# Modulation vectors of the attention stages moved from TensorE to VectorE, in one queue through ten stages, with half of one projection placed between two attention heads

## The chip, the cores and the metric

One core of a Trainium2 chip runs the whole program. The metric is device microseconds of one execution, the median of several runs. TensorE (PE in the profile; PEld is its weight load) does the matmuls, VectorE (DVE) and ScalarE (ACT) the elementwise work, and SyncE (SP) issues the loads from HBM. Each engine works its own instructions off in one fixed order.

## The reference, cut to what matters

Two networks run one after the other on x of 256 tokens by 1024 features, in ten stages. The first has two layers of feed-forward, attention, feed-forward; the second two layers of mixer, feed-forward. Every stage i has the same frame:

```
sh, sc, g = split(silu(c) @ w_mod + b_mod)           # vectors of 1024
h = rms_norm(x) * gain * (1 + sc) + sh
x = x + g * block(h)
```

So the program needs 30 vectors of 1024 numbers, sh, sc and g of ten stages, and each is a product of a vector of 1024 with a 1024x1024 matrix of 4 MB. They hang on c alone, not on x, and can be worked out at any time before their use. An attention block has six latent heads (queries and keys are expanded from a narrow latent), six local heads (a window of 128 with a bias table, two key heads) and four stick-breaking heads; their outputs are normed by branch and projected by w_out.

## The kernel before

**Weights.** Every projection streams its weight through `wblocks` (lines 177 to 207) in blocks of 128 partitions by 1024 numbers. Line 186 issues the load of a block into a `raw` buffer; there are six of these, and feed-forward stages from the second on have six more (`rawx`). ScalarE rounds the block to `whi` (line 197), VectorE takes the rest `wlo = raw - whi` (line 198), and TensorE multiplies with both halves: lines 218, 231 and 235 where the weight is stationary (24 matmuls of 256 columns a block), 262, 263 and 265 where the activation is (12 matmuls of up to 512 columns a block). A feed-forward stage has 66 such blocks, a mixer 64.

**Vectors.** The matrix of one vector comes as eight row blocks ("rows" from here on) of 128x1024, 512 KB each, through the same `raw` buffers (line 437). `queue_vec` (from line 429) has two ways to use a row. In mode "dve" VectorE does `acc = acc + cond[k] * row`, line 452 for the first row and 454 for the others, and after eight rows `vec_row` sums over partitions with four matmuls against ones (line 481). In mode "pe" TensorE does the whole sum: four matmuls of 32 output rows by 256 columns for each row (line 447), all into the one PSUM bank `gv`. The profile counts each of these fp32 matmuls as two instructions, so eight for a row. In both modes ScalarE copies the sum to `vrow` (line 488), two matmuls transpose it (line 496), and VectorE adds the bias (line 500): `finish_vec`. The set-up's two vectors use "pe", the two attention stages use "pe" as well, all others "dve".

**Pacing.** `stage` queues a stage's vectors, and `pace` is called after each weight block and takes as many rows as keep them evenly spread: from block 4 to block 53 of a feed-forward, to block 57 of a mixer. The stages use 24, 24, 32, 24, 16, 32, 24, 24, 24 and 0 rows, 224 in all. In attention the pacing is by hand: after each head's second half `advance` takes three rows (`f3`) or one (`f1`), and `q` in `PLAN` takes what is left.

**Attention** (from line 1223). Projections come first; the local heads' projection of 512 columns (`proj_n(win, (416, 928), op)`, four blocks) stands between `up_proj` and `mla_prep`, which norms, rotates and transposes the latent queries and keys. Then `PLAN` orders the heads: `m` a latent head and `s` a local one, `S` the local heads' preparation `swa_prep`, `B` a branch's norm and transposition, `a` and `b` parts of the w_out projection, `d` how many heads are kept open. Each head has a first half (scores, maximum, exponential) and a second half (transposes, weighted sum).

```
PLAN = "d2 f3 m0 m1 d3 S B2 s0 f1 s1 s5 m3 m2 s3 s4 s2 a6 m4 m5 w B1 a4 b6 q B0 b4"
```

The order in which each engine gets its instructions is made by a scheduler: an instruction that stands later in the program can be put ahead of one that waits, as far as its buffers allow.

Of the kernel before, what the change touches and what calls it, by code (L numbers as in the profile page):

```python
# [9 lines left out]
F32 = mybir.dt.float32  # L10
# [27 lines left out]
PFFN = 53  # L38
PATT = 18
PLAN = "d2 f3 m0 m1 d3 S B2 s0 f1 s1 s5 m3 m2 s3 s4 s2 a6 m4 m5 w B1 a4 b6 q B0 b4"  # L40
PRE = (0, 0, 0, 0)
DEPTH = 3
PMIX = 57
GAIN_EARLY = (3, 4, 6, 7, 8, 9)
# [4 lines left out]
SH_MODE = "pe"  # L49
# [8 lines left out]
AHEAD_MORE = 4  # L58
AHEAD_PE = 1
# [72 lines left out]
class Net:  # L132
    def __init__(self, ctx, tc, A, out, offs, dbg=None):
# [11 lines left out]
        self.more, self.nraw, self.finishing = None, 0, None  # L145

# [240 lines left out]
    def stage(self, nblk, vecs, mode="dve", quiet=0, flush=False, apart=True, ahead=AHEAD):  # L387

        self.drain()
        for v in vecs:  # L390
            self.queue_vec(mode, *v, apart=apart)
        if apart:
            self.finish_last()
        elif flush:
            self.loads.append(None)
            self.steps.append(self.finish_last)
        self.total, self.ahead = len(self.steps), ahead
        self.done, self.nload, self.nblk, self.iblk = 0, 0, max(1, nblk - quiet), -quiet
        if ahead > AHEAD:
            self.preload(ahead)  # L400
# [5 lines left out]
    def next_step(self):  # L406

        self.preload(self.done + 1 + self.ahead)
        self.steps.pop(0)()
        self.done += 1  # L410
# [7 lines left out]

    def pace(self):
        if self.manual:  # L420
            return
        if self.later and self.iblk >= T5_WAIT and self.iblk % T5_EVERY == 0:
            self.later.pop(0)()
        self.iblk += 1
        want = min(self.total, -(-self.iblk * self.total // self.nblk))
        while self.done < want:
            self.next_step()

    def queue_vec(self, mode, w, col0, cond, cols, kind, key, apart):
# [3 lines left out]
        def load(b):  # L433
            raw = self.raw()
            m = LD // D
            rv = raw.rearrange("p (k n) -> p k n", k=m)
            nc.sync.dma_start(rv, w[b * P : (b + m) * P, col0 : col0 + D].rearrange("(k p) n -> p k n", p=P))
            for k in range(m):
                st[b + k] = rv[:, k, :]

        def use(b):
            if b == 0:
                st["acc"] = self.t(self.vp, [P, D], F32, "acc", 2) if mode == "dve" else self.gv()
            acc, row, k = st["acc"], st.pop(b), b
            if mode == "pe":
                for g in range(4):
                    nc.tensor.matmul(  # L447
                        acc[32 * g : 32 * g + 32, 0:S], lhsT=self.cond[cond][1][:, k, :], rhs=row[:, g * S : (g + 1) * S],
                        start=k == 0, stop=k == 7,
                    )  # L450
            elif k == 0:
                nc.vector.tensor_scalar(out=acc, in0=row, scalar1=self.cond[cond][0][:, 0:1], scalar2=None, op0=ALU.mult)
            else:
                nc.vector.scalar_tensor_tensor(  # L454
                    out=acc, in0=row, scalar=self.cond[cond][0][:, k : k + 1], in1=acc, op0=ALU.mult, op1=ALU.add
                )
            if b == 7:
                st["row"] = self.vec_row(mode, acc)
                if not apart:
                    self.finishing = lambda bank: self.finish_vec(st["row"], cols, kind, key, bank)  # L460

        for b in range(8):
# [515 lines left out]
    def stage_vecs(self, i):  # L978
# [5 lines left out]
        if i in GAIN_EARLY:  # L984
            keys = keys[1:]
# [797 lines left out]
```

## Time and profile before

| | |
|---|---|
| median of 3 runs | 1904.32 us |
| runs | 1897.71 to 1905.79 us |
| profiled execution, its own time | 1893.67 us |
| its span, first to last instruction | 1891.9 us |
| PE busy | 97% of the span |
| DVE busy | 72% |
| ACT busy | 51% |
| attention stages, about | 245 to 375 us and 766 to 890 us |
| mixers, about | 1090 to 1308 us and 1492 to 1710 us |

The profile shows one execution. Busy shares are means over stages with different limits. A matmul's end is modelled, so the time that a run of matmuls takes of PE is read from start to start. PEclk is the clock that TensorE was granted, as a share of 2.4 GHz: 1.00 or 0.50.

### The profile page before, as it was taken

How to read it: one execution, taken by the hardware profiler on the slowest of the kernel's cores; microseconds unless marked ns; L12 is line 12 of the kernel's file. 1: busy time of each engine (PE TensorE's matmuls, PEld its weight loads, DVE VectorE, ACT ScalarE, POOL GpSimd, SP SyncE). 2: the span in 40 equal slices, each digit the busy share in tenths (PEclk: the TensorE clock that was granted, in tenths of full speed). 3: DMA queues.
4: the chain of work that ended last, by engine and by line, in shares of the span. 5: the costliest groups of instructions: out<-in, count | busy, mean ns of one | idle time of the engine just before them, and what ended most of it. 6: DMA issues, size and time to landing. Idle time of an engine off the chain costs nothing.

```text
span 1891.9 us, 37147 instructions
## 1 busy us (share of the span) xinstructions
PE 1839.9 (97%) x15125; PEld 1736.0 (92%) x15125; DVE 1371.3 (72%) x2171; ACT 960.2 (51%) x1527; POOL 0.2 (0%) x4
## 2 busy tenths in 40 slices
PE   7999999999999999999999999999999999999998
PEld 5899996899999999968999988999999888999998
DVE  4897576698669765768986696679865777577554
ACT  3444475554445444756544454546444545455443
POOL 0000000000000000000000000000000000000000
PEclk8999999999999999999999999999999999999999
DMA  9698545789857963458798477578984585775550
GB/s 319 195 331 288 187 141 191 267 279 378 283 178 274 319 230 118 135 190 296 249 340 269 157 250 235 195 233 281 337 267 147 189 295 178 248 252 186 195 191 23
DMA packets 229447, 440.72 MB, mean 233 GB/s; under 512 B 15590, under 2 KB 79708, under 8 KB 229276
## 3 DMA queue, kind: packets, MB, share of 16 engines
q1 hardware_dynamic: 227740, 436.96, 68.0%
q8 instruction: 118, 1.93, 0.4%
q10 hardware_dynamic: 1536, 1.39, 0.2%
q14 instruction: 53, 0.43, 0.1%
HBM read 436.06 MB, written 2.23 MB: 232 GB/s over the span
## 4 chain that ended last, share of the span: by engine, by line
PE 87%; DVE 6%; DMA 3%; ACT 2%; issue 1%; SPq 0%; DVEq 0%; ACTq 0%
PE mm L218 24%; PE mm L235 23%; PE mm L231 23%; DVE wlo L198 2%; PE mm L262 2%; PE mm L265 2%; PE mm L263 2%; PE gv L447 2%; PE sm L771 1%; ACT whi L197 1%; DMA raw<-in_w_ffn_gu_dram 1%; PE mm L771 1%; PE gv L481 1%; DMA rawx<-in_w_mod_dram 1%; DMA raw<-in_w_mod_dram 1%
## 5 line engine op out<-in xcount | busy, mean ns | idle before, releaser
L218 PE MATMUL mm<-oph,whi 128*128 128x256 f32 (+1 forms) x3072 | 786.3, 282 | 13.3 <-DVE dly L302 4.9
L231 PE MATMUL mm<-opl,whi 128*128 128x256 f32 (+1 forms) x3072 | 780.0, 280 | 0.1
L197 ACT ACTIVATE whi<-raw 128x1024 fp32r<-128x1024 f32 (+2 forms) x408 | 426.2, 1047 | 455.4 <-PE mm L231 352.1
L198 DVE TENSOR_TENSOR wlo<-raw,whi 128x1024 fp32r<-128x1024 f32 (+2 forms) x408 | 489.8, 1208 | 176.5 <-ACT whi L197 168.5
L218 PEld LDWEIGHTS mm<-oph,whi 128*128 128x128 f32 x3072 | 582.5, 190 | 30.1 <-issue 10.3
L231 PEld LDWEIGHTS mm<-opl,whi 128*128 128x128 f32 x3072 | 582.6, 190 | 2.2 <-issue 0.9
L235 PE MATMUL mm<-oph,wlo 128*128 128x256 f32 (+1 forms) x3072 | 574.8, 280 | 8.6 <-DVE wlo L198 8.4
L235 PEld LDWEIGHTS mm<-oph,wlo 128*128 128x128 f32 x3072 | 453.9, 190 | 12.2 <-DVE wlo L198 11.1
L197 ACT ACTIVATE whi<-rawx 128x1024 fp32r<-128x1024 f32 x160 | 170.1, 1064 | 193.8 <-PE mm L231 159.0
L218 PE MATMUL mm<-ah,whi 128*128 128x256 f32 x1056 | 268.1, 278 | 0.0
L231 PE MATMUL mm<-al,whi 128*128 128x256 f32 x1056 | 267.0, 277 | 0.0
L198 DVE TENSOR_TENSOR wlo<-rawx,whi 128x1024 fp32r<-128x1024 f32 x160 | 194.8, 1223 | 91.3 <-ACT whi L197 90.6
L454 DVE SCALAR_TENSOR_TENSOR acc<-raw,silc,acc 128x1024 f32<-128x1024 f32 x119 | 152.5, 1283 | 77.9 <-DMA raw<-in_w_ada_dram 60.4
L235 PE MATMUL mm<-ah,wlo 128*128 128x256 f32 x1056 | 206.8, 277 | 0.7 <-DVE wlo L198 0.7
L218 PEld LDWEIGHTS mm<-ah,whi 128*128 128x128 f32 x1056 | 198.4, 188 | 3.0 <-issue 2.5
L231 PEld LDWEIGHTS mm<-al,whi 128*128 128x128 f32 x1056 | 198.5, 188 | 0.0
L235 PEld LDWEIGHTS mm<-ah,wlo 128*128 128x128 f32 x1056 | 159.5, 188 | 1.1 <-DVE wlo L198 1.1
L262 PE MATMUL mm<-whi,oph 128*128 128x512 f32 (+2 forms) x192 | 73.9, 388 | 0.3 <-ACT oph L640 0.2
L263 PE MATMUL mm<-whi,opl 128*128 128x512 f32 (+2 forms) x192 | 73.0, 380 | 0.0
L454 DVE SCALAR_TENSOR_TENSOR acc<-rawx,silc,acc 128x1024 f32<-128x1024 f32 x42 | 53.9, 1283 | 18.3 <-DMA rawx<-in_w_ada_dram 9.3
L698 ACT ACTIVATE ah<-sil 128x512 fp32r<-128x512 f32 x66 | 40.3, 624 | 37.0 <-DVE sil L760 29.7
L265 PE MATMUL mm<-wlo,oph 128*128 128x512 f32 (+2 forms) x192 | 56.6, 378 | 0.0
(374 smaller groups left out, 1660.3 us busy)
## 6 DMA issues: line engine op xcount, KB each, us to landing
raw<-in_w_mod_dram SPq DMA_DIRECT2D x119, 512.0 KB
raw<-in_w_ffn_gu_dram SPq DMA_DIRECT2D x104, 512.0 KB
raw<-in_w_in_dram SPq DMA_DIRECT2D x104, 512.0 KB
raw<-in_w_ada_dram SPq DMA_DIRECT2D x75, 512.0 KB
rawx<-in_w_ffn_gu_dram SPq DMA_DIRECT2D x64, 512.0 KB
raw<-in_w_ffn_down_dram SPq DMA_DIRECT2D x54, 512.0 KB
raw<-in_w_ffn_in_dram SPq DMA_DIRECT2D x48, 512.0 KB
rawx<-in_w_ffn_in_dram SPq DMA_DIRECT2D x40, 512.0 KB
```

Source lines behind the costliest of these rows:

```text
L197: nc.scalar.activation(out=whi[:, :tot], in_=src, func=AF.Copy)
L198: nc.vector.tensor_tensor(out=wlo[:, :tot], in0=src, in1=whi[:, :tot].bitcast(F32), op=ALU.subtract)
L218: i0 = nc.tensor.matmul(o, lhsT=whi[:, k, cs], rhs=xhi[:, kop0 + k, :ncol], start=zero and (opener or not shared), stop=False, **kw)
L231: nc.tensor.matmul(o, lhsT=whi[:, k, cs], rhs=xlo[:, kop0 + k, :ncol], start=False, stop=False, **kw)
L235: nc.tensor.matmul(o, lhsT=wlo[:, k, cs], rhs=xhi[:, kop0 + k, :ncol], start=False, stop=last and k == nk - 1, **kw)
L262: nc.tensor.matmul(o, lhsT=xhi[:, kop0 + k, ts], rhs=whi[:, k, cols], start=first and k == 0, stop=False)
L263: nc.tensor.matmul(o, lhsT=xlo[:, kop0 + k, ts], rhs=whi[:, k, cols], start=False, stop=False)
L265: nc.tensor.matmul(o, lhsT=xhi[:, kop0 + k, ts], rhs=wlo[:, k, cols], start=False, stop=last and k == nk - 1)
L447: nc.tensor.matmul(acc[32 * g : 32 * g + 32, 0:S], lhsT=self.cond[cond][1][:, k, :], rhs=row[:, g * S : (g + 1) * S], start=k == 0, stop=k ...
L454: nc.vector.scalar_tensor_tensor(out=acc, in0=row, scalar=self.cond[cond][0][:, k : k + 1], in1=acc, op0=ALU.mult, op1=ALU.add)
L698: nc.scalar.activation(out=hi, in_=src, func=AF.Copy)
L771: self.nc.tensor.transpose(out, in_, self.ident[:n, :n])
```

## The change

All 28 vectors after the set-up's two go into one list of 224 rows (`vloads`, `vuses`), made before the first stage. `begin` sets for a stage how many rows of the list are to be used by a block called due (`USES[i][0]`) and by the stage's end (`USES[i][1]`); `vec_uses` takes rows, always on VectorE, and `vec_loads` keeps loads ahead (three in attention and mixers, five in feed-forwards after the first). Rows by stage become 30, 18, 36, 28, 8, 36, 16, 32, 16 and 4. The due block of a feed-forward is 53 and of a mixer 57 as before; the rest of a stage's rows now follow between due and end. In attention the rows are spread over the heads' second halves (`HEADS` = 13 against twelve heads), and `require` takes what is missing before the residual. `queue_vec` stays for the set-up, on TensorE.

In attention the local heads' projection is a generator `swa_proj`: two blocks of it stay ahead of `mla_prep`, the third stands after `m0` and the fourth after `m1` (`p` in `PLAN`). The `f` and `q` entries are gone.

```
-PLAN = "d2 f3 m0 m1 d3 S B2 s0 f1 s1 s5 m3 m2 s3 s4 s2 a6 m4 m5 w B1 a4 b6 q B0 b4"
+PLAN = "d2 m0 p m1 p d3 S B2 s0 s1 s5 m3 m2 s3 s4 s2 a6 m4 m5 w B1 a4 b6 B0 b4"
+HEADS = 13
-GAIN_EARLY = (3, 4, 6, 7, 8, 9)
+USES = ((24, 30), (48, 48), (80, 84), (104, 112), (120, 120), (152, 156), (168, 172), (200, 204), (216, 220), (224, 224))
+DUE = {"ffn": 53, "attn": 0, "mix": 57}
...
+    def begin(self, i, kind, nblk):
+        due, end = USES[i]
+        self.ffn_now, self.iblk = kind == "ffn", 0
+        at = DUE[kind] - (66 - nblk if kind == "ffn" else 0)
+        self.rise = ((QUIET, self.used), (at, due), (nblk, end))
+        self.limit, self.vahead = end, AHEAD_MORE if kind == "ffn" and i else AHEAD
+        if not self.ffn_now:
+            self.finish_last()
+        elif i:
+            self.vec_loads(self.used + self.vahead)
...
+    def vec_uses(self, n):
+        while self.used < min(n, self.limit):
+            if not self.ffn_now:
+                self.finish_last()
+            self.vec_loads(self.used + 1 + self.vahead)
+            self.vuses[self.used]()
+            self.used += 1
+
+    def require(self, i):
+        self.vec_uses(USES[i][0])
+        last = ("sh", i + 1) if i + 1 < len(self.order) else ("g", i)
+        if last not in self.cols:
+            self.finish_last()
...
     def pace(self):
...
+        for (a, m), (b, n) in zip(self.rise, self.rise[1:]):
+            if a < self.iblk <= b:
+                self.vec_uses(m - (m - n) * (self.iblk - a) // (b - a))
...
+    def add_vec(self, w, col0, cond, cols, kind, key):
...
+            by = self.cond[cond][0][:, b : b + 1]
+            if b == 0:
+                nc.vector.tensor_scalar(out=acc, in0=row, scalar1=by, scalar2=None, op0=ALU.mult)
             else:
+                nc.vector.scalar_tensor_tensor(out=acc, in0=row, scalar=by, in1=acc, op0=ALU.mult, op1=ALU.add)
             if b == 7:
+                st["row"] = self.vec_row("dve", acc)
+                self.finishing = lambda bank: self.finish_vec(st["row"], cols, kind, key, bank)
...
-            pq = self.proj_n(win, (416, 928), op)
...
+            swa = self.swa_proj(win, op, sqk)
+            next(swa)
+            next(swa)
...
+                elif kind == "p":
+                    next(swa)
...
             f(st)
-            self.advance(fill)
+            self.nhead += 1
+            self.vec_uses(self.used0 + (USES[i][0] - self.used0) * self.nhead // HEADS)
...
+    def swa_proj(self, win, op, sqk):
+        nc = self.nc
+        pq = [self.mm(), self.mm()]
+        for wb, k0, q in self.wblocks(win, 0, 8, 416, 512):
+            self.mm_n(pq, wb, op, q, k0, k0 == 0, k0 + q == 8, slice(0, 512))
...
+            yield
...
             for c in range(2):
                 self.residual(4 * c, self.proj_t(wdn, c * 512, (ahi, alo), nk=22), i)
+            self.vec_uses(self.limit)
```

## Rows read from the trace of the kernel before

**Rows 1.** The page: engines' busy time, and the chain that ended last by engine
```profile
PE 1839.9 (97%) x15125; PEld 1736.0 (92%) x15125; DVE 1371.3 (72%) x2171; ACT 960.2 (51%) x1527; POOL 0.2 (0%) x4
...
PE 87%; DVE 6%; DMA 3%; ACT 2%; issue 1%; SPq 0%; DVEq 0%; ACTq 0%
```

**Rows 2.** Windows: stretch and length, busy us of each engine, PEclk, DMA share, GB/s
```profile
245.00:375.00 130.00, 127.21 (x932) 103.82 (x931) 86.09 (x239) 81.27 (x207) 0.00 (x0) 0.99 0.59 201
...
766.00:890.00 124.00, 120.79 (x860) 99.59 (x859) 90.19 (x247) 82.52 (x209) 0.00 (x0) 1.00 0.61 201
...
1308.00:1492.00 184.00, 184.00 (x1617) 182.43 (x1617) 133.88 (x165) 91.05 (x122) 0.00 (x0) 1.00 0.70 238
```

**Rows 3.** Windows for line 447 alone, both attention stages: PE, PEld busy
```profile
245.00:375.00 130.00, 18.16 (x192) 5.80 (x192) 0.99 0.59 201
766.00:890.00 124.00, 13.48 (x128) 3.91 (x128) 1.00 0.61 201
```

**Rows 4.** Timeline near the first attention's end: start, us, engine, line, operation
```profile
352.28 2.79 PE L447 MATMUL gv<-raw,repc 128*32 128x256 f32 x46
352.97 3.44 SPq L186 DMA_DIRECT2D raw<-in_w_out_dram  x5
...
355.00 0.66 PE L771 MATMUL sm<-ident,mix 128*128 128x128 f32 x4
...
357.20 1.06 ACT L197 ACTIVATE whi<-raw 128x1024 fp32r<-128x1024 f32 x1 [0.24 <-DMA raw<-in_w_out_dram]
...
358.31 0.39 PE L218 MATMUL mm<-oph,whi 128*128 128x256 f32 x1 [1.86 <-ACT whi L197]
```

**Rows 5.** Windows just behind that, and in the first mixer
```profile
359.60:363.00 3.40, 3.40 (x16) 3.40 (x17) 2.88 (x5) 1.84 (x4) 0.00 (x0) 0.51 0.93 337
...
1168.60:1172.00 3.40, 3.16 (x13) 3.00 (x14) 1.19 (x3) 0.00 (x0) 0.00 (x0) 0.50 0.80 285
```

**Rows 6.** Windows: the heads of each attention stage, and ahead of the first
```profile
299.50:345.00 45.50, 44.75 (x359) 29.32 (x358) 29.00 (x107) 26.23 (x87) 0.00 (x0) 1.00 0.69 247
820.30:866.00 45.70, 44.50 (x356) 29.83 (x355) 30.26 (x110) 27.66 (x90) 0.00 (x0) 1.00 0.70 246
281.90:299.50 17.60, 17.57 (x102) 14.81 (x101) 10.01 (x19) 10.46 (x20) 0.00 (x0) 1.00 0.38 120
```

**Rows 7.** Lines 454 and 481: count, ns least/median/most, first and last start
```profile
L454 DVE SCALAR_TENSOR_TENSOR acc<-raw,silc,acc x119: 1276/1283/1292, 82.3 to 1645.1; 128x1024 f32<-128x1024 f32 x119
...
L481 PE MATMUL gv<-acc,ones x184: 379/391/404, 113.3 to 1663.9; 128*32 128x256 f32 x184
```

**Rows 8.** SP's timeline, 270 to 290 us, and line 447's first use
```profile
270.17 17.67 SPq L437 DMA_DIRECT2D raw<-in_w_mod_dram  x6
...
L447 PE MATMUL gv<-raw,repc x192: 379/379/404, 301.2 to 354.7; 128*32 128x256 f32 x192
```

**Rows 9.** Timeline: the local projection, the latent and the local heads' preparation
```profile
281.92 0.39 PE L262 MATMUL mm<-whi,oph 128*128 128x512 f32 x1
...
282.55 1.23 DVE L198 TENSOR_TENSOR wlo<-raw,whi 128x1024 fp32r<-128x1024 f32 x1 [0.50 <-ACT whi L197]
...
291.43 0.62 DVE L1404 TENSOR_TENSOR kn<-kr,r3y 128x192 f32<-128x192 f32 x2
...
292.45 0.63 PE L265 MATMUL mm<-wlo,oph 128*128 128x512 f32 x2
...
299.78 1.06 ACT L1433 ACTIVATE kn<-sqk 128x1024 f32<-128x1024 f32 x1 [0.78 <-ACT qT L1419]
...
312.78 0.48 PE L1505 MATMUL sm<-qkT 64*128 64x128 f32 x2
```

**Rows 10.** Timeline in the first mixer, and VectorE's wait over the program
```profile
1165.85 1.28 DVE L454 SCALAR_TENSOR_TENSOR acc<-raw,silc,acc 128x1024 f32<-128x1024 f32 x1 [2.56 <-DMA raw<-in_w_ada_dram]
...
1168.84 0.77 PE L1599 MATMUL sm<-slotB,dec 128*128 128x128 f32 x2 [2.10 <-issue]
...
DVE acc L454 <- DMA raw<-in_w_ada_dram: 60.4, 27, 4.2
```

More of the change, by code (lines that the diff above doesn't have):

```diff
@@ L48 @@
 T5_HELD = (0,)*10
-SH_MODE = "pe"
 LO_AT = 3
@@ L385, in proj_n, with stage @@
         return outs
-    def stage(self, nblk, vecs, mode="dve", quiet=0, flush=False, apart=True, ahead=AHEAD):
+    def stage(self, vecs):
         self.drain()
         for v in vecs:
[L391 to L400, printed above, removed]
+            self.queue_vec(*v)
+        self.done, self.nload = 0, 0
     def drain(self):
@@ L422, in pace @@
-        if self.later and self.iblk >= T5_WAIT and self.iblk % T5_EVERY == 0:
+        if self.later and self.iblk >= T5_WAIT + QUIET and self.iblk % T5_EVERY == 0:
             self.later.pop(0)()
         self.iblk += 1
[L425 to L429, printed above, removed]
+        if self.manual or self.rise is None:
+            return
+        if not self.ffn_now:
+            self.finish_last()
@@ L430, in queue_vec @@
+    def queue_vec(self, w, col0, cond, cols, kind, key):
         nc = self.nc
         st = {}
[L433 to L439, printed above, removed]
         def use(b):
             if b == 0:
[L443 to L455, printed above, removed]
@@ L456, in use @@
+                st["acc"] = self.gv()
+            row = st.pop(b)
+            for g in range(4):
+                nc.tensor.matmul(
+                    st["acc"][32 * g : 32 * g + 32, 0:S], lhsT=self.cond[cond][1][:, b, :],
+                    rhs=row[:, g * S : (g + 1) * S], start=b == 0, stop=b == 7,
                 )
             if b == 7:
-                st["row"] = self.vec_row(mode, acc)
-                if not apart:
-                    self.finishing = lambda bank: self.finish_vec(st["row"], cols, kind, key, bank)
@@ L462, in queue_vec @@
-        for b in range(8):
-            self.loads.append((lambda b=b: load(b)) if b % (LD // D) == 0 else None)
-            self.steps.append(lambda b=b: use(b))
-        if apart:
-            self.loads.append(None)
-            self.steps.append(lambda: self.finish_vec(st["row"], cols, kind, key))
+                st["row"] = self.vec_row("pe", st["acc"])
+        self.loads += self.vec_load(w, col0, st) + [None]
+        self.steps += [lambda b=b: use(b) for b in range(8)]
+        self.steps.append(lambda: self.finish_vec(st["row"], cols, kind, key))
@@ L835, in setup @@
             self.xa = self.operand(width=S + 2)
-            self.stage(1, [self.vec("sc", 0)], "pe", ahead=AHEAD_PE)
+            self.stage([self.vec("sc", 0)])
             self.preload(3)
@@ L854, in setup @@
             self.drain()
-            self.stage(1, [self.vec("sh", 0)], SH_MODE, ahead=AHEAD_PE)
+            self.stage([self.vec("sh", 0)])
             held.high(0)
@@ L981, in own @@
             return out + ([("sc", i + 1), ("sh", i + 1)] if i + 1 < len(self.order) else [])
[L983 to L988 removed]
+        return [self.vec(*k) for k in own(i)]
     def bias_loads(self, pool):
@@ L1718, in build @@
         first_parts = self.setup(tmp)
-        quiet = {"ffn": QUIET, "attn": 0, "mix": QUIET}
-        pacing = {"ffn": PFFN, "attn": PATT, "mix": PMIX}
+        blocks = {"ffn": 66, "attn": 27, "mix": 64}
+        for i in range(len(self.order)):
+            for v in self.stage_vecs(i):
+                self.add_vec(*v)
         for i, (blk, l, m) in enumerate(self.order):
@@ L1728, in build @@
                 held = first_parts
-            self.stage(
-                pacing[kind] - (8 if i == 0 else 0), self.stage_vecs(i), "pe" if kind == "attn" else "dve", quiet[kind],
-                flush=i == 0, apart=kind != "ffn", ahead=AHEAD_PE if kind == "attn" else (AHEAD_MORE if kind == "ffn" and i else AHEAD),
-            )
+            self.begin(i, kind, blocks[kind] - (10 if i == 0 else 0))
             if kind == "ffn":
```

80 lines of the change are left out of this document (44 added, 36 removed).

## The prediction

> **What bounds the kernel now.** I read the page first. PE is busy for 97% of the span and 87% of the chain that ended last is PE; VectorE has 72% of the span and 6% of the chain [rows 1]. So time is won by taking work off TensorE, or by closing one of its few waits, and VectorE has room on average. An average doesn't say where, so I cut the span into stages. A feed-forward late in the program shows PE busy for 184.00 of 184 us with VectorE at 133.88 [rows 2]: there nothing can be won, and rows added there are hidden as long as VectorE stays ahead. The attention stages are where TensorE does something that VectorE could do, the vector sums of line 447 [rows 3], so the argument is about them, and above all about the stretch of the heads, where both engines work in short turns.
>
> **Part 1: what leaves TensorE.** The attention stages hold 192 and 128 instructions of line 447 [rows 3]. Their spans of 18.16 and 13.48 us include waits, for other instructions stand between them. The price without waits comes from a run of 46: it starts at 352.28 and the next PE instruction starts at 355.00, so 2.72 us or 59 ns each, 0.47 us for a row's eight [rows 4]. All 320 are 18.9 us. What comes back is the sum over partitions: 184 instructions of line 481 are 23 vectors at eight each [rows 7], and now there are 28, so 5 x 8 x 59 ns = 2.4 us more.
>
> **Part 2: the heads of the first attention.** Of the 192 instructions, 46 lie behind the heads, and 138 in the heads' 45.5 us (8.1 us of PE). In that stretch VectorE is busy for 29.0 us [rows 6], so it idles for 16.5. After the change 16 of the stage's 18 rows (12 of 13 shares) belong there, at up to 1.28 us each [rows 7], so 20.5 us, and with them two wlo of the moved projection at 1.23 us [rows 9], 2.5 us. That makes 52.0 us. Some of it can run earlier. SP had issued six row loads by 288 us [rows 8], while line 447 starts only at 301 [rows 3]: rows lie ready before the heads begin. Ahead of the heads VectorE works 10.0 of 17.6 us [rows 6]; without the two moved blocks that stretch is 5.5 us shorter (four blocks run from 281.92 to 292.9, so 2.75 each [rows 9]) and 2.5 us lighter, which leaves 4.6 us, three rows. VectorE then has 48.2 us, and PE has 45.5 - 8.1 + 5.5 = 42.9. The stretch that took 45.5 + 5.5 = 51.0 takes about 48.2, set by VectorE instead of PE: 2.8 us won. The ends: 52.0 with no row ahead (1.0 us lost), 42.9 if VectorE gets wholly out of the way (8.1 won). I stay near the first, since VectorE's order is fixed and its work there comes in turns with the others.
>
> **Part 3: the end of the first attention.** The 46 drained instructions stand before the transposes of the last branch, whose source is ready. While they run their rows hold `raw` buffers: SP issues five w_out loads only from 352.97, ScalarE gets the first at 357.20, and PE waits 1.86 us until 358.31 [rows 4]. Then the clock stands at 0.51 for 3.4 us [rows 5], half speed, so 1.7 us more. Together 2.7 + 1.9 + 1.7 = 6.3. Against this, two rows are left for `require`, 2.6 us on VectorE in front of the residual; its loads are issued three rows ahead, so I charge half, 1.3: 5.0 us won. The ends are 2.7 (the loads come late anyway) and 6.3.
>
> The Trainium skill (TensorE: Matmul & The Clock Gate, Part 1) says that the half clock is the default and that activity releases it. The trace agrees: 0.51 right behind a wait of 1.86 us. The rule speaks against the change, for the line-447 work is activity that covers waits among the heads; by the row alone the end of the stage gains, by the rule the heads may give that back, which the third case below prices from rows.
>
> **Part 4: the second attention.** Only eight rows are left, seven of them among the heads. VectorE: 30.3 + 7 x 1.28 + 2.5 - 3.8 (three rows ahead) = 38.0 us. PE: 45.7 - 128 x 59 ns + 5.5 = 43.6 against 45.7 + 5.5 = 51.2, so PE bounds and up to 7.6 us are free. But the local heads' preparation takes 13.0 us in the first attention (299.78 to 312.78 [rows 9]), and it can now begin only behind the fourth projection block, which therefore can't cover it. The chain is 29% of the heads' 45.5 us, and line 447 was cover for it; I let the same share of the 7.6 us come back as idle time, 2.2, so 5.4 us are won (ends 0 and 7.6). In the first attention VectorE's 48.2 us already hold that much slack for PE. Taking the moved blocks from before `mla_prep` costs nothing by the rows: its keys are ready at 292.05 (291.43 + 0.62 [rows 9]), the four blocks ended at 292.9, and without two of them PE has two stick-breaking heads to finish and the queries to transpose. If that cover failed it would be up to 2.5 us a stage, which I leave to the range.
>
> **Part 5: mixers.** They use 16 rows where they used 24. In the first mixer an acc waits 2.56 us for its row's load, a product that line 1599 needs is queued behind it on VectorE, PE idles 2.10 us [rows 10], and the clock stands at 0.50 for 3.4 us [rows 5]: 3.8 us. Over the program such waits on the second network's rows add up to 60.4 us of VectorE in 27 waits [rows 10], most of them covered. With a third fewer rows I let 2.5 us of such a stall go in each mixer, 5 in all (ends 0 and 7.6).
>
> **Part 6: feed-forwards and tails.** The stage of 184 us gets eight rows more: 133.9 + 10.2 = 144 us of VectorE [rows 2, 7], still 78%, hidden behind PE. New is that 34 rows in seven stages follow the due block, where none did. A block is 2.8 us of matmuls (184 us over 66 blocks [rows 2]) with 1.23 us of wlo [rows 9], so a row fits. What isn't covered is a row that VectorE starts just when the residual's additions become ready, on which the next stage's operand hangs: at most 1.28 us at each of seven ends, 9.0 us. I take 0.5 each, 3.5.
>
> **Sum.** -2.8 - 5.0 - 5.4 - 5.0 + 3.5 + 2.4 = -12.3 us. On the profiled execution's 1893.7 that gives 1881.4. This execution lies 10.6 us below the median of the runs, so on the median the same difference gives 1904.3 - 12.3 = 1892.0 us.
>
> **The rivals.**
>
> *All of it comes back.* Rows find VectorE's gaps and the scheduler puts other matmuls where line 447 was. Then 18.9 us go, with 3.6 at the stage's end (wait and clock; the drain is in the 18.9) and up to 7.6 in the mixers, less 2.4: 27.7, so 1877. For it: 16.5 us of VectorE's idle time among the heads. Against it: 18 rows are more than that.
>
> *The work of line 447 was free.* It filled waits that stay: heads hang on each other's turns of PE, ScalarE and VectorE whatever PE does meanwhile. Then parts 2 and 4 give nothing, and -5.0 - 5.0 + 3.5 + 2.4 = -4.1, so 1900. If every attention adds two waits like those of rows 4 and 10, the clock halves for 3.4 us behind each, 1.7 us a time, 6.8 together: 1907. For it: line 447's spans in rows 3 are 12.7 us longer than its price, and that is waiting. Against it: the last 46 instructions of it in the first stage cover nothing [rows 4].
>
> *A row in front of a head (slower).* VectorE takes a row of 1.28 us just before a head's maximum, sum or weighted sum becomes ready; PE, without its filler, waits for that head. There are 24 heads. Parts 2 and 4 are lost (8.2), and each head delayed by one row on the path costs 1.28: with half the heads 15.4, so 1892.0 + 8.2 + 15.4 = 1916; with all, 1931. From eleven heads on the kernel is slower by more than 0.5%. For it: VectorE's sum of 52.0 us in part 2 leaves it little slack in the first attention. Against it: in the second it has slack, and the heads stand earlier in the program than most rows.
>
> **How the numbers follow.** The forecast has 0.46, all of it back 0.18, the free filler 0.20, the row in front of a head 0.16. The median of this kernel moves by about half a per cent without cause, so 0.5% (9.5 us) is the bound: faster is under 1894.8, slower over 1913.8. The forecast spreads from 1884 to 1899 by its own ends, 0.36 of it faster and 0.10 not; with the second case's 0.18 and 0.02 of the third that is 0.56 faster; 0.28 the same (0.10, 0.17 and 0.01 of the fourth); 0.16 slower (0.01 and 0.15). The range leaves out about a tenth on each side: down to 1876, the second case whole, and up to 1914, a good half of the fourth's way. The forecast's own range is 1884 to 1899.
>
> **What would show it.** No line 447 behind the set-up; 28 vectors at line 481. In the first attention VectorE busier than 45 us in the stretch of the heads, and a stretch of about 48 us from the first scores to the last weighted sum; in the second one of about 46. The wait of 1.86 us and the half clock at the first attention's end gone. Attention stages shorter by about 8 and 5 us, mixers by 2 to 3, feed-forwards equal or half a microsecond longer at their ends. The prediction is wrong if heads wait on VectorE rows one by one (PE idle in pieces of a microsecond, half clock among the heads), if the tails' rows stand in front of the residuals, or if the w_out loads still come late.

## The result and the profile after

The changed kernel takes 1919.89 us (median of four executions, 1914.79 to 1933.29), the kernel before beside it 1903.38 (1897.71 to 1905.79): ratio 1.0108, 95% interval 1.0076 to 1.014. It is slower by 1.1%; the forecast was 0.6% faster. Ratios and intervals here and below leave out executions more than 1.5% above the fastest of the same kernel (of the experiments below one each of no_filler, dve_only and no_tail, two of att_rows_out), while medians and ranges hold all executions.

Each execution comes with TensorE's mean granted clock as a share of 2.4 GHz: 0.986 to 0.995 in the 78 executions of the kernel before that ran beside the experiments, but 0.964, 0.968, 0.976 and 0.975 in the four of the changed one, the lowest in the longest. The profile is that of the execution of 1933.29 us. Three lines of its page: busy time, the granted clock in 40 slices (tenths), the chain that ended last.

```profile
PE 1861.3 (96%) x14845; PEld 1767.6 (92%) x14845; DVE 1412.7 (73%) x2211; ACT 958.0 (50%) x1527; POOL 0.2 (0%) x4
...
PEclk8999998799999999976999999999999999999999
...
PE 77%; DVE 8%; DMA 8%; ACT 4%; issue 2%; SPq 0%; DVEq 0%; ACTq 0%
```

TensorE executes 280 instructions fewer than in [rows 1] and is busy 21 us longer. PE's part of the chain went from 87% to 77%. Behind the program's start the clock has two dents, slices 7 and 8 and slices 18 and 19, each of 48.3 us: the heads of the two attention stages.

Next, windows of the kernel before and after with the columns of [rows 2]. Before: the first attention from the residual in front of it to its own, the second likewise, the last 69.8 us of the first feed-forward, the last 80.8 us of the one ahead of the second attention, and the two mixers.

```profile
239.80:376.50 136.70, 133.44 (x980) 109.66 (x978) 92.75 (x259) 86.00 (x216) 0.00 (x0) 0.99 0.59 198
759.80:891.90 132.10, 128.89 (x928) 107.69 (x927) 97.16 (x263) 87.15 (x215) 0.00 (x0) 1.00 0.60 199
...
170.00:239.80 69.80, 69.62 (x604) 67.39 (x604) 43.76 (x64) 31.66 (x44) 0.00 (x0) 1.00 0.69 222
679.00:759.80 80.80, 80.80 (x716) 80.37 (x715) 46.12 (x58) 37.64 (x49) 0.00 (x0) 1.00 0.46 151
...
1083.40:1295.40 212.00, 206.63 (x1569) 192.36 (x1568) 160.23 (x228) 104.12 (x150) 0.00 (x0) 0.99 0.71 238
1484.10:1698.00 213.90, 206.25 (x1556) 191.71 (x1555) 157.31 (x223) 103.21 (x150) 0.00 (x0) 0.98 0.71 240
```

After, the same stretches; between them the heads of the first attention, and in the second one the 6.6 us from its first scores and the 37.4 us behind them.

```profile
249.80:392.70 142.90, 133.82 (x812) 116.96 (x811) 113.77 (x276) 84.96 (x214) 0.00 (x0) 0.86 0.59 189
308.80:366.00 57.20, 49.30 (x244) 38.45 (x243) 40.48 (x116) 27.14 (x89) 0.00 (x0) 0.68 0.49 157
...
781.00:929.30 148.30, 138.18 (x808) 121.68 (x807) 105.96 (x270) 87.40 (x215) 0.00 (x0) 0.83 0.49 159
...
845.00:851.60 6.60, 3.89 (x23) 2.45 (x21) 5.82 (x14) 5.38 (x15) 0.00 (x0) 1.00 0.33 110
851.70:889.10 37.40, 36.24 (x142) 27.82 (x142) 19.08 (x69) 13.48 (x51) 0.00 (x0) 0.50 0.27 89
...
180.00:249.80 69.80, 65.79 (x554) 63.94 (x555) 44.30 (x65) 29.33 (x41) 0.00 (x0) 0.98 0.73 235
700.00:781.00 81.00, 78.00 (x688) 76.75 (x688) 50.74 (x63) 35.90 (x49) 0.00 (x0) 1.00 0.57 183
...
1121.80:1331.20 209.40, 204.54 (x1552) 191.09 (x1550) 152.51 (x220) 102.87 (x149) 0.00 (x0) 0.99 0.69 226
1525.30:1736.10 210.80, 207.57 (x1554) 194.44 (x1554) 151.27 (x219) 103.44 (x149) 0.00 (x0) 0.99 0.68 220
```

Three things stand in these rows. The attention stages grew by 6.2 and 16.2 us, with 168 and 120 instructions fewer on TensorE and a mean clock of 0.86 and 0.83; the pauses of TensorE in the two together went from 6.5 to 19.2 us. The ends of the two feed-forwards, where TensorE hardly paused before, have 4.0 us of pause in 69.8 and 3.0 in 81.0; the first feed-forward as a whole ends at 249.8 us where it ended at 239.8. The mixers became 2.6 and 3.1 us shorter.

**How the clock falls.** TensorE's timeline in the second attention, at two latent heads and the last moved block's product:

```profile
846.74 0.47 PE L264 MATMUL mm<-wlo,oph 128*128 128x512 f32 x1
848.24 0.33 PE L816 MATMUL mm<-ident,P 128*128 128x128 f32 x1 [1.02 <-ACT P L1201]
848.78 0.44 PE L816 MATMUL mm<-ident,P 128*128 128x128 f32 x2 [0.22 <-ACT P L1201]
850.48 0.33 PE L816 MATMUL mm<-ident,P 128*128 128x128 f32 x1 [1.25 <-ACT P L1201]
851.02 0.44 PE L816 MATMUL mm<-ident,P 128*128 128x128 f32 x2 [0.22 <-ACT P L1201]
...
851.70 0.63 PE L1180 MATMUL mm<-kvraw,PT 128*128 128x64 f32 x2
```

With both heads' scores done, TensorE waits four times within 5 us, 2.7 us in all, for ScalarE's exponentials. Right behind, at 851.7, the clock stands at 0.50, and stays there for 37.4 us in which TensorE is busy for 36.24: from start to start its work now takes about twice as long (from line 1180 to line 1181 0.42 us at 851.70, 0.22 at 889.88 when the clock is back), so the heads fill TensorE at 1.2 GHz. No wait in this stretch is long; what is lost there is that the same work runs at half speed. In the kernel before, the heads ran at 1.00 throughout [rows 6], and line 447 stood in these very waits. TensorE's timeline there, in the first attention, between the transposes of the first two latent heads' exponentials (P):

```profile
301.22 1.48 PE L447 MATMUL gv<-raw,repc 128*32 128x256 f32 x18
302.63 0.33 PE L771 MATMUL mm<-ident,P 128*128 128x128 f32 x1
302.89 0.64 PE L447 MATMUL gv<-raw,repc 128*32 128x256 f32 x8
303.46 0.44 PE L771 MATMUL mm<-ident,P 128*128 128x128 f32 x2
303.83 1.07 PE L447 MATMUL gv<-raw,repc 128*32 128x256 f32 x16
```

In its whole profile the kernel before has no wait of TensorE for these exponentials; the changed one has eight, 4.9 us in all. The latent heads' scores show the clock by themselves (their modelled times, least, median, most ns), before and after:

```profile
L1525 PE MATMUL sm<-kT,qT x24: 379/380/382, 299.8 to 853.6; 96*128 96x256 f32 x24
```

```profile
L1567 PE MATMUL sm<-kT,qT x24: 379/508/635, 309.0 to 886.9; 96*128 96x256 f32 x24
```

**How the moved blocks and a row meet.** Timelines of TensorE, VectorE and ScalarE of the changed kernel, around the local heads' preparation in the first attention:

```profile
318.62 0.96 PE L537 MATMUL gv<-cst,vrow 128*128 128x4 f32 x4
322.92 1.97 PE L816 MATMUL sm<-ident,sqk 128*128 128x128 f32 x8 [3.33 <-DVE sqk L1478]
...
319.08 0.17 DVE L1157 TENSOR_SCALAR r2v<-ss 128x16 f32<-128x16 f32 x1
...
319.71 1.28 DVE L502 SCALAR_TENSOR_TENSOR acc<-raw,silc,acc 128x1024 f32<-128x1024 f32 x1
320.90 0.17 DVE L604 TENSOR_TENSOR r2t<-r2y 128x16 f32<-128x16 f32 x1
...
321.64 1.22 DVE L1478 TENSOR_TENSOR sqk<-sqk,r2y 128x1024 f32<-128x1024 f32 x1
...
314.50 1.10 ACT L1475 ACTIVATE kn<-sqk 128x1024 f32<-128x1024 f32 x1
...
319.42 0.20 ACT L598 ACTIVATE r2y<-r2y 128x16 f32<-128x16 f32 x1
```

The preparation starts at 314.50, where it started at 299.78 [rows 9], since the projection's last block now stands behind m1. The value that VectorE needs is there at 319.62, a row of line 502 holds VectorE from 319.71 to 320.99, and TensorE, with nothing left to do, waits 3.33 us. The row is 1.3 us of that; the rest is the preparation itself, which now lies open.

**The tails.** VectorE's and TensorE's timelines in the end of the first feed-forward, and VectorE's in the other one:

```profile
192.15 1.28 DVE L502 SCALAR_TENSOR_TENSOR acc<-raw,silc,acc 128x1024 f32<-128x1024 f32 x1 [4.95 <-DMA raw<-in_w_mod_dram]
193.35 2.35 DVE L197 TENSOR_TENSOR wlo<-raw,whi 128x1024 fp32r<-128x1024 f32 x2
...
194.63 0.51 PE L234 MATMUL mm<-ah,wlo 128*128 128x256 f32 x2 [1.57 <-DVE wlo L197]
...
719.13 1.28 DVE L502 SCALAR_TENSOR_TENSOR acc<-raw,silc,acc 128x1024 f32<-128x1024 f32 x1 [4.74 <-DMA raw<-in_w_mod_dram]
```

A row whose load hasn't come stands at the head of VectorE's queue for 4.95 us; two wlo that TensorE needs are behind it, and TensorE waits for the first.

### The profile page after: what moved, and what is told of

Read it like the earlier page. It is cut to its first block, busy times and chain, and to the rows that moved or that the text cites. A ratio compares the mean times of both kernels' runs of the same rounds, so it can differ in the third digit from the quotient of the medians.

```text
span 1931.3 us, 36618 instructions
## 1 busy us (share of the span) xinstructions
PE 1861.3 (96%) x14845; PEld 1767.6 (92%) x14845; DVE 1412.7 (73%) x2211; ACT 958.0 (50%) x1527; POOL 0.2 (0%) x4
## 4 chain that ended last, share of the span: by engine, by line
PE 77%; DVE 8%; DMA 8%; ACT 4%; issue 2%; SPq 0%; DVEq 0%; ACTq 0%
PE mm L217 21%; PE mm L234 21%; PE mm L230 21%; DMA raw<-in_w_mod_dram 4%; DVE wlo L197 3%; PE mm L261 2%; PE mm L262 2%; PE mm L264 2%; ACT whi L196 2%; DMA raw<-in_w_ada_dram 1%; DMA rawx<-in_w_mod_dram 1%; DVE acc L502 1%; PE gv L522 1%; PE sm L816 1%; PE mm L816 1%
## 5 line engine op out<-in xcount | busy, mean ns | idle before, releaser
L217 PEld LDWEIGHTS mm<-oph,whi 128*128 128x128 f32 x3072 | 588.4, 192 | 31.4 <-issue 12.1
L234 PEld LDWEIGHTS mm<-oph,wlo 128*128 128x128 f32 x3072 | 457.5, 191 | 10.1 <-DVE wlo L197 9.5
L502 DVE SCALAR_TENSOR_TENSOR acc<-raw,silc,acc 128x1024 f32<-128x1024 f32 x145 | 185.5, 1281 | 78.5 <-DMA raw<-in_w_mod_dram 42.3
L197 DVE TENSOR_TENSOR wlo<-rawx,whi 128x1024 fp32r<-128x1024 f32 x157 | 190.6, 1221 | 63.0 <-ACT whi L196 62.8
L502 DVE SCALAR_TENSOR_TENSOR acc<-rawx,silc,acc 128x1024 f32<-128x1024 f32 x51 | 65.3, 1280 | 32.3 <-DMA rawx<-in_w_mod_dram 22.0
L745 ACT ACTIVATE oph<-x,colsc 128x256 fp32r<-128x256 f32 x80 | 38.5, 498 | 40.1 <-DVE x L715 39.5
```

Source lines behind the costliest of these rows:

```text
L197: nc.vector.tensor_tensor(out=wlo[:, :tot], in0=src, in1=whi[:, :tot].bitcast(F32), op=ALU.subtract)
L217: i0 = nc.tensor.matmul(o, lhsT=whi[:, k, cs], rhs=xhi[:, kop0 + k, :ncol], start=zero and (opener or not shared), stop=False, **kw)
L234: nc.tensor.matmul(o, lhsT=wlo[:, k, cs], rhs=xhi[:, kop0 + k, :ncol], start=False, stop=last and k == nk - 1, **kw)
L502: nc.vector.scalar_tensor_tensor(out=acc, in0=row, scalar=by, in1=acc, op0=ALU.mult, op1=ALU.add)
L745: nc.scalar.activation(out=hi, in_=src, func=AF.Identity, scale=gain)
```

## The experiments

Three things changed together: line 447 left the heads (with rows on VectorE in its place), half a projection moved in between two heads, rows moved into the tails. Each was tried alone, and some in pairs. Medians are of the executions that belong to each kernel, ratios are to the kernel before on the same chip (1900.79, 1903.27 and 1901.95 us for the three sets of four).

The changed kernel itself was timed in the four executions above alone, and executions of one kernel lie up to 42 us apart, so a difference between two of these medians is uncertain by some 10 us. Most of that spread goes with the clock: within one kernel, on average over the changed one and the twelve below, an execution is 1.6 us longer for each 0.001 that its mean clock is lower. "At an equal clock" below means that each execution's time was moved by this price to a clock of 0.980 and the mean taken; such differences are estimates, uncertain by some 3 us.

### Line 447 taken out, and work put in its place

**no_filler**: the kernel before without the attention stages' rows but the first of each vector: 35 rows neither loaded nor multiplied, nothing on VectorE in their place, nothing moved.

```
...
             acc, row, k = st["acc"], st.pop(b, None), b
+            if mode == "pe" and self.manual_next:
+                if b == 0:
...
+            elif mode == "pe":
...
+            skip = b > 0 and mode == "pe" and self.manual_next
+            self.loads.append(None if skip else (lambda b=b: load(b)))
```

> The kernel before with line 447's work left out of the attention stages but for the first row of each vector (21 + 14 rows neither loaded nor multiplied, so these vectors are wrong): 280 TensorE instructions of 59 ns less, 16.5 us, and no VectorE row in their place. If that work was a load on TensorE, the kernel gains 12 to 20 us. If it was filler that kept the clock up, the attentions get no shorter or get longer (132 us or more each) and show 20 us or more of half clock each, though they do less.

Measured: 1897.78 us (1880.43 to 1922.22, ten executions), ratio 0.9965 (0.993 to 1.0). The two executions with a mean clock of 0.990 and 0.989 took 1881.89 and 1880.43 us, the one with 0.963 took 1922.22: about 1.6 us for each 0.001 of clock. The seven others have clocks of 0.973 to 0.982, where the kernel before beside them has 0.988 to 0.993. The profile is that of the longest. Two windows of it, in the heads of each attention stage:

```profile
304.60:342.00 37.40, 36.75 (x145) 27.22 (x144) 16.98 (x68) 14.32 (x55) 0.00 (x0) 0.50 0.26 75
833.70:871.00 37.30, 36.57 (x140) 27.78 (x140) 18.16 (x68) 14.14 (x54) 0.00 (x0) 0.50 0.25 75
```

So the heads lose the clock without a row on VectorE in front of them (in these two stages the first addition on VectorE starts at 326.48 and 839.72 us, behind the fall) and without a moved block. Both theories of the expectation come out in part: at the clock of the kernel before, taking the work and its loads out is worth some 20 us, where its price says 16.5, and the clock takes most of it back in most executions. A fall of 0.001 in the mean clock is 3.8 us more at half speed in 1900, so 0.42 us are lost for each of these, near the half that it would be if TensorE bounded all of it.

**dve_only**: the kernel before with the attention stages' rows on VectorE.

```
-... "pe" if kind == "attn" else "dve", ...
+... "dve", ...
```

> The kernel before with the other part alone: the attentions' vectors on VectorE (24 and 16 rows there, more than the changed kernel's 18 and 8), pacing, stages and projection as before. If the missing TensorE work lets the clock fall, this kernel shows it too: a mean clock of 0.98 or less and times that spread over 20 us or more from run to run, the slow ones at the low clock, with a median of 1900 to 1920. If the one queue or the moved projection is the cause, it keeps the clock of before (0.99) and gains 10 us or more.

Measured: 1915.79 us (1895.82 to 1925.29, ten), ratio 1.0056 (1.0022 to 1.009), mean clocks 0.966 to 0.985. Its profile, of an execution at 0.976, has 6.7 and 10.1 us at half clock in the heads of the first attention and 23.7 and 13.5 in the second. Nothing else of the change is in it, and by the ratios it loses half of what the change loses, with 40 rows on VectorE in the attention stages where the change has 26. Against no_filler, which has 40 rows less on VectorE, it is 18 us longer; by 1.6 us for 0.001, the medians of their clocks (0.9745 and 0.980) account for 9 of these, and the rows with their loads for the rest.

**filler_back**: the changed kernel with useless matmuls behind each head's second half, 224 instructions in the two stages.

```
+            self.filler(st[0], 3 if self.nhead == 0 else 1)
...
```

> The changed kernel with TensorE work of no use behind each head's second half (three rows' worth behind the first, one behind the other eleven: 14 x 8 instructions, 6.6 us a stage; nothing reads the sums). If the missing filler is the cause, half clock in the attentions falls from 92 us to under 30, each attention is 8 us or more shorter, and the kernel falls to about 1900 or less, although it does more. If VectorE's rows are the cause, it stays at 1915 or rises by up to 13 us.

Measured: 1925.59 us (1922.47 to 1933.5, four), ratio 1.0151 (1.012 to 1.0182). The clock came half the way back (0.980 to 0.984, from 0.964 to 0.976; 0.988 to 0.993 before), with only matmuls added. The time didn't, and the 1900 us of the expectation was missed: at an equal clock it is 23 us longer than the changed kernel, so the added work costs more than its 224 x 59 ns = 13.2 us and eats what the clock gives. What part of that is the bank that it shares with the vectors' sums wasn't told apart.

**a6_early**: the changed kernel with no rows in the tails (as no_tail below), and real work as filler: the two w_out blocks of `a6` behind local heads 0, 1 and 5.

```
-PLAN = "... s0 s1 s5 m3 m2 s3 s4 s2 a6 m4 ..."
+PLAN = "... s0 s1 s5 a6 m3 m2 s3 s4 s2 m4 ..."
```

> The changed kernel without rows behind the due block, and with the w_out blocks that need only the first two branches (a6) placed behind local heads 0, 1 and 5 instead of behind all local heads. Against the kernel without the tail rows alone (1911.4, mean clock 0.965 to 0.981). Theory A (the heads lack filler for TensorE): real work there instead of line 447 raises the mean clock above 0.98 and the time falls by 5 us or more. Theory B (any work of TensorE among the heads costs its own time, and the latent heads behind it now lack it): within 4 us either way.

Measured: 1900.12 us (1894.58 to 1903.19, ten), ratio 0.9991 (0.9971 to 1.0012): 11.3 us less than no_tail, and executions that lie within 9 us of each other, not 35. But the clock is 0.972 to 0.980, where over 0.98 was expected. The time speaks for the theory, the clock rose by too little (0.971 to 0.9755, worth 7 us) to be all of it; what the rest is wasn't tried.

### The rows on VectorE

**att_rows_out**: the changed kernel without the attention stages' rows but the first of each vector, 23 in all neither loaded nor added.

```
...
+        out = [b > 0 and (30 <= n0 + b < 48 or 112 <= n0 + b < 120) for b in range(8)]
+        self.vloads += [None if o else f for o, f in zip(out, self.vec_load(w, col0, st))]
...
```

> The changed kernel with all but the first row of each vector left out of the two attention stages (16 + 7 rows neither loaded nor added, so these three vectors are wrong). In the changed kernel the attentions took 143.0 and 148.3 us (136.8 and 132.1 before), 41 and 51 us of it at half clock. If VectorE's rows in front of the heads are the cause, the attentions fall to 125 to 132 us each with hardly any half clock, and the kernel to 1890 or less. If the missing TensorE work among the heads is the cause, rows or not, they stay at 135 us or more with 20 us or more of half clock each.

Measured: 1897.72 us (1891.04 to 1921.63, ten), ratio 0.9986 (0.9957 to 1.0014). 22 us less than the changed kernel, but only 4 at an equal clock; clocks from 0.969 to 0.987. In its profile, at 0.983, the attention stages take 129.4 and 133.2 us, one inside the first theory's 125 to 132, the other between it and the second's 135. So beside the late projection the rows do harm, by the clock for the most part, but without them the clock still falls.

**rows_out_whole**: the same with the projection whole again ahead of `mla_prep` (the edit of swa_whole below).

> The changed kernel with the projection whole ahead of mla_prep and with all rows of the two attention stages but the first of each vector neither loaded nor added, 23 rows in all. Against the kernel with the whole projection alone (1903.4) this takes the rows of VectorE out of the heads. Theory A (without line 447 the heads lose the clock by themselves; the rows matter little): half clock of 15 to 50 us stays in the heads, time 1890 to 1902. Theory B (a row in front of a head is what makes the heads wait): the half clock goes nearly away, under 8 us, and the time falls by 15 us or more, to 1888 or less.

Measured: 1902.51 us (1890.46 to 1913.34, ten), ratio 0.9999 (0.9969 to 1.003). Against swa_whole (1903.38, below), which has these rows, 0.9 us: nothing that could be told from noise, close to the first theory's 1890 to 1902. Its attention stages, in the columns of [rows 2]:

```profile
247.80:374.80 127.00, 121.46 (x825) 107.46 (x825) 97.75 (x266) 86.92 (x216) 0.00 (x0) 0.97 0.52 160
760.60:900.20 139.60, 134.64 (x808) 118.07 (x807) 97.79 (x263) 87.82 (x215) 0.00 (x0) 0.85 0.46 142
```

One stage nearly kept its clock, the other lost it, in one execution of one kernel. Four or five additions are left among the heads of each stage, first rows and rows of the next stage that the scheduler put ahead; but in the second stage the clock falls at about 827 us, ahead of the first whole addition of 1.28 us at 831.05. So the clock falls without such a row in front of a head. With the projection whole the 23 rows cost nothing that shows, with half of it late 22 us: the two do harm together, and 319.71 above shows one such meeting.

### The moved half of the projection

**swa_whole**: the changed kernel with the projection whole ahead of `mla_prep`.

```
-PLAN = "d2 m0 p m1 p d3 ..."
+PLAN = "d2 m0 m1 d3 ..."
-            next(swa)
-            next(swa)
+            for _ in swa:
+                pass
```

> The changed kernel with the local heads' projection whole again, ahead of the latent heads' preparation. The moved half was 5.5 us of TensorE work among the first heads, cover that would now be gone: by the theory of missing filler the clock falls further or stays (0.965 to 0.975) and the time stays at 1915 to 1930. If the moved half is what delays the local heads, the time falls by 8 us or more.

Measured: 1903.38 us (1890.06 to 1915.61, ten), ratio 0.9996 (0.9959 to 1.0034): 16.5 us less than the changed kernel. The theory that the moved half is filler expected 1915 to 1930 and missed. The waits of TensorE for the local heads' preparation (us, times, longest) are 3.3, 1, 3.3 in the changed kernel; in this one:

```profile
PE sm L816 <- DVE sqk L1478: 1.4, 1, 1.4
```

The wait is 1.9 us shorter, the rest comes through the clock: its median is 0.983 against 0.9715, 18 us by 1.6 for 0.001, and at an equal clock the two kernels are 3 us apart. How the late half lowers the clock isn't shown.

**half_moved**: the kernel before, line 447 kept, with the projection in halves as in the change.

```
-PLAN = "d2 f3 m0 m1 d3 ..."
+PLAN = "d2 f3 m0 p m1 p d3 ..."
...
```

> The kernel before with one part of the change alone: half of the local heads' projection between m0 and m1; vectors as before, on TensorE in attention. If the half clock comes from TensorE's missing rows, the clock stays at 0.985 or more and the time within 0.5% of before. If moving the projection is itself harmful (TensorE waits for the latent keys ahead of the heads, or for the local heads' preparation behind), the attentions grow by 3 us or more each and the kernel by 6 us or more.

Measured: 1898.13 us (1893.07 to 1909.55, ten), ratio 0.9979 (0.9958 to 1.0), clock 0.988 to 0.993. With line 447 there to fill, the move does no harm and may give 5 us (4 at an equal clock). The same edit costs 16 us in one kernel and nothing in the other.

### The tails

**no_tail**: the changed kernel with all rows of a stage due at its due block.

```
-USES = ((24, 30), (48, 48), (80, 84), (104, 112), ...
+USES = ((30, 30), (48, 48), (84, 84), (112, 112), ...
```

> The changed kernel with the same rows in each stage, but all of them due at the block that the kernel before used (43 in the first, 53 in feed-forwards, 57 in mixers), none behind it. In the changed kernel an acc that waits 2.7 to 4.9 us for its row holds wlo behind it near the ends of feed-forwards. If that is what makes stages one, four and eight longer (10.0, 5.0 and 5.4 us), these fall by 3 us or more each and the kernel by 8 to 15 us. If those stages are longer because they hold more rows at all, the time stays within 5 us of the changed kernel's.

Measured: 1911.38 us (1893.53 to 1928.36, ten), ratio 1.0035 (0.9999 to 1.0071): 8.5 us less than the changed kernel, at the same median clock (0.971); at an equal clock 9 us. The two ends, in the columns of [rows 2]:

```profile
171.00:240.80 69.80, 69.80 (x604) 68.42 (x605) 44.75 (x64) 30.67 (x43) 0.00 (x0) 1.00 0.74 239
679.40:760.20 80.80, 80.80 (x717) 80.37 (x716) 46.88 (x60) 37.76 (x49) 0.00 (x0) 1.00 0.51 159
```

TensorE has no pause left in them, though as many rows run in the stage. In the first of them VectorE waits 0.2 us once for a row of the first network, where in the changed kernel it waits six times, 14.4 us in all. Only the rows' place was wrong.

### Together

**whole_no_tail**: both undone.

> The changed kernel with two parts undone together: the rows that follow the due block come before it again, and the local heads' projection stands whole ahead of mla_prep. Undone alone, the projection gave 16.5 us (1919.9 to 1903.4) and the rows 8.5 us (to 1911.4). Theory A (three separate causes: late row loads in the tails, the projection, the clock in the heads): the two add to 25 us, so 1890 to 1900, with stages 0, 3 and 7 near 240, 191 and 189 us and the half clock in the heads between 10 and 40 us per execution. Theory B (both only moved the one clock's fall): no more than the larger of the two, so 1900 to 1908.

Measured: 1894.04 us (1884.36 to 1909.29, ten), ratio 0.996 (0.9931 to 0.9988). From no_tail to this one the projection gives 17.3 us (16.5 in the first pair), from swa_whole the tails give 9.3 (8.5): the two add up, as the first theory had it (1890 to 1900), and what is left of the change is a little faster than before. At an equal clock the tails are worth 9 and 8 us in the two pairs and the projection 3 and 1: the tails cost time by themselves, the projection by the clock. The clock is still 0.976 to 0.987.

**gain_late**: the kernel before with only the vectors' order changed: the mixers' rows go from 24 to 16 each, and two feed-forwards take 8 more.

```
-GAIN_EARLY = (3, 4, 6, 7, 8, 9)
+GAIN_EARLY = (3, 4, 6, 8)
-flush=i == 0, ...
+flush=i in (0, 9), ...
```

> The kernel before with the vectors' order changed alone: g of the seventh and of the tenth stage one stage later, so that mixers use 16 rows and not 24, and two feed-forwards 32 and 8; nothing moves in attention. In the changed kernel the two mixers are 2.7 and 3.2 us shorter than before while the last two feed-forwards are longer. If that gain in the mixers is the fewer rows', this kernel is 3 to 7 us faster than before, at the same clock. If it is not, it stays within 2 us.

Measured: 1887.99 us (1887.0 to 1895.11, seven), ratio 0.9938 (0.9916 to 0.9961), clock 0.988 to 0.993. That is 15.3 us, where 3 to 7 were expected. It keeps line 447 and is 6 us faster than whole_no_tail, which doesn't (within the uncertainty of two medians).

**late_half**: the last with the projection in halves (half_moved).

> The kernel before, line 447 kept, with three of the gain vectors late (16 rows in each mixer, as in the changed kernel) and half of the local heads' projection between the latent heads 0 and 1. Alone the first gave 1888.0 and the second 1898.1, against 1901 to 1904. Theory A (the half is harmless, and worth some 5 us, as long as line 447 stands in the heads): the two add, 1880 to 1886. Theory B (the half is worth nothing): 1886 to 1891.

Measured: 1881.07 us (1877.47 to 1890.53, four), ratio 0.9894 (0.9856 to 0.9932), clock 0.993 to 0.995. That is in the first theory's range. This version beats both kernels. Its attention stages and mixers:

```profile
239.20:373.10 133.90, 130.25 (x983) 108.15 (x983) 92.36 (x258) 85.42 (x214) 0.00 (x0) 1.00 0.63 203
757.30:889.40 132.10, 127.03 (x932) 107.85 (x931) 97.46 (x264) 87.36 (x216) 0.00 (x0) 1.00 0.65 206
1080.70:1286.50 205.80, 203.79 (x1560) 190.53 (x1559) 151.19 (x219) 103.74 (x149) 0.00 (x0) 1.00 0.70 226
1474.90:1680.70 205.80, 204.06 (x1562) 190.82 (x1561) 151.25 (x218) 103.70 (x149) 0.00 (x0) 1.00 0.70 226
```

The clock is 1.00 in all four.

## Why the prediction was wrong

The step that failed is parts 2 and 4, the heads, and in them a term put at nothing without a reason: that the heads would go on at 2.4 GHz when line 447 left them. The median clock went from 0.991 to 0.9715, which is 31 us by the price of 1.6 us for 0.001. The rival "the work of line 447 was free" named the mechanism and mis-sized it: two waits an attention with the clock halved for 3.4 us behind each, 6.8 us in all. In the profiled execution, the longest of the four, the first attention has three stretches at half clock, from 315.8, 332.9 and 360.2 us, 10.1, 20.3 and 10.1 long, the second one three, of 3.4, 37.4 and 10.1: 91.4 us together. The rows that the price was taken from [rows 5] show 3.4 us behind each wait. Why it lasts longer among the heads isn't shown: TensorE has no pause at all in the stretch of 20.3 us and 1.2 us of them in that of 37.4, so further pauses can't account for it.

At an equal clock the changed kernel is 12 us shorter than the kernel before, which is the forecast's sum of 12.3; this is an estimate, since no execution of the one has a clock that the other had. The agreement is luck in part, since the parts missed both ways: the tails took more than was charged, and taking line 447 out gave more (24 us for no_filler at an equal clock, its loads among them).

**Part 1** was right. no_filler leaves out 280 of the 320 instructions, 16.5 us at 59 ns, and its two executions at an unchanged clock are 19 and 20 us shorter than the median before, with the loads of these rows gone as well. All 224 instructions of line 522 (481 before) stand in the trace, the 28 vectors.

**Part 2** forecast 48.2 us for the heads, bound by VectorE at more than 45 us. They take 57.2 with VectorE at 40.48 and the clock at 0.68. Ten of the stage's 18 rows fall into them, where 13 were counted; the other eight ran ahead. VectorE was not the bound, and its sum says nothing about who waits for whom or at what clock.

**Part 3** was right about the wait: the 1.86 us of [rows 4] are 0.24 now, and the drain is gone. The 1.7 us of clock weren't won: 10.1 us from 360.2, across the end of the heads, stand at 0.50. The sentence on the Trainium skill (TensorE: Matmul & The Clock Gate, Part 1) that the half clock is the default and activity releases it was set beside the row and left to a rival of 0.20; what it warned of, half clock in the heads, is what decided. The same page's section "A second HAM failure mode: psum-queue depth-cycling" comes nearer: it tells of a kernel that lost clock through frequent short idle pieces between groups of matmuls rather than through one long wait. The trace agrees on how the clock falls: four waits of 0.22 to 1.25 us stand in front of 37.4 us at 0.50. It doesn't on what follows: there the clock went up and down between the two levels, here it stayed low for 37.4 us.

**Part 4** gave 5.4 us and called the moved blocks free, with 2.5 us a stage if not. They cost 16.5 and 17.3 us in the two pairs. The error was to ask only whether the latent keys would be ready, and to price the late preparation as idle time and not as clock. The local heads' preparation starts 14.7 us later (299.78 to 314.50), of which 10.0 are the stage's own delay, and a row of VectorE came in its way with TensorE idle, 1.3 us of a wait of 3.33. All but 1 to 3 us of the cost goes with the clock.

**Part 5** was right in this kernel: 2.6 and 3.1 us against 5 in all. By itself the edit is worth more: 15.3 us in gain_late (12 at an equal clock), and the mixers of late_half are 205.8 us each against 212.0 and 213.9, 14.3 us together. Why the changed kernel's mixers keep 3.6 and 5.0 us of that wasn't tried.

**Part 6** gave 3.5 us for a row in front of the residual, at most 9.0. The tails cost 8.5 and 9.3 us by another mechanism: VectorE holds at a row whose load is late, with wlo behind it. The prediction priced the addition and not the load. Why the loads come late wasn't tried; between 170 and 250 us SyncE in its turn waits 15 times, 24.2 us in all, for wlo before it can issue a weight's load. The Trainium skill (DVE: scalar operands, raw-bit mode, write accounting and state across instructions, section 5) says that VectorE's queue is one in-order queue; the 4.95 us wait with two wlo behind it is that rule at work.

The third rival, a row in front of a head, named nearly the right time (1916) for a reason that holds only in part, so that was luck: rows cost 9 of the 18 us between dve_only and no_filler, and 22 us with the late projection (4 at an equal clock), but nothing with the projection whole.

What stays open: why one execution of a kernel keeps the clock in a stage and the next doesn't; what holds the clock down once it has fallen; and how the late half of the projection lowers it.

## What to carry to other kernels

Before taking work off the busiest engine, ask whether it was filling waits of a chain that stays: read the granted clock of that stretch, and try the kernel with the work left out and nothing put in its place, several times, looking at the spread and not only the median. An edit that is harmless beside the filler can cost 16 us without it, so parts of a change are tried alone and in pairs. Where weights stream through the same buffers, a row that may be late doesn't belong at the head of the queue that also makes the weights ready.

## What was not expected of the hardware

The heads can stay at half clock for 37.4 us at a stretch with TensorE busy for 36.24 of it, and the same kernel does so in one execution and not in another: no_filler ran at 1880 us with a mean clock of 0.989 and at 1906 us with 0.974 (and once at 1922 with 0.963), while the kernel before stayed between 1895 and 1911 beside it. TensorE's busy share says nothing of this; 96% in the changed kernel is partly the same work at 1.2 GHz.
